# Moving half of the gate projection to the end of the in-projection, with the first attention pairs between its tiles

## The chip, the cores and the metric

The kernel runs on one core of one Trainium2 chip. The metric is the device time of one execution in microseconds. Three runs of the kernel before gave 1553.62, 1555.27 and 1555.58 us, so its median is 1555.27 us.

## The reference, cut to what matters

One layer of a diffusion backbone over 1024 latent and 256 context tokens (1280 in all), model width 1024. After adaLN modulation and RMSNorm, ONE input projection feeds two groups:

```python
p   = h @ w_in                                   # columns: q k v (3*512) | z (512) | a,b (16) | nq nk nv (3*512)
# group A, 4 heads of 128: gated DeltaNet, forward and backward scans summed
q, k, v = split(silu(conv5(p[q k v])))           # depthwise convolution over the tokens, 5 taps
q = l2norm(q) / sqrt(128);  k = l2norm(k)
v_new = u - w @ S;  o = (q*exp(g)) @ S + qk @ v_new;  S = S*exp(g_last) + k_dec.T @ v_new   # per chunk
oA = rmsnorm(o_f + o_b) * silu(z)                # z: the output gates
# group B, 8 heads of 64: neighbourhood attention, 8x16 window plus all context keys, one softmax
oB = softmax(rms(nq) @ rms(nk).T + bias) @ nv
x = x + gate * (concat(oA, oB) @ w_out);  then RMSNorm, SwiGLU, gated residual
```

The group A scans need q, k, v and, per chunk, an inverted triangular matrix; the gates z are wanted only when a chunk's two scans are both done.

## The kernel before, in words

All fp32 products are made of three fp32r products of split operands (`hi` and `lo` parts), so each logical product is three matmuls. `hh` and `hl` are the two parts of the normalised input, eight tiles of 128 x 1280 each, held in SBUF for the whole in-projection.

**The job list.** The in-projection is a list of jobs, run in order by the loop at line 1032. A `Block` (line 405) makes 128 output columns over all tokens, channel-major: 8 k-steps of 9 matmuls (6 where only latent tokens are wanted: `q` and `nq`). Its matmuls are recorded at line 402. Kinds `q`, `k`, `v` then go through `evac` (ScalarE copies to `cr` at line 450, five VectorE operations at lines 454 and 458 for the convolution), `silu` (line 465) and, one job later, `finish` (PE transposes at line 524, VectorE scaling into `vt` at line 528, a store to DRAM). Kinds `nq`, `nk` go through a norm (line 489 on). A `Wide` (line 561) makes 256 columns token-major, one tile of 128 tokens at a time, 24 matmuls a tile (line 585): `z` for the gates (8 latent tiles), `nv` for the attention's values (10 tiles). Its weights are fetched in two halves through one buffer `wraw`: a DMA (line 576), a ScalarE cast to `hi` (line 577), a GpSimd subtraction to `lo` (line 578).

The order before is `k0 k1 k2 k3 z1 | nk0 nk1 nk2 z0 nk3 | nq0 nq1 nq2 q0 q1 q2 q3 | nv0 v0 nv1 v1 v2 v3 nq3`.

**What runs beside the jobs.** `bg` steps two background pieces between k-steps and tiles: the block inverses (from the sixth job on), then `preps` (line 905), which prepares ten chunks for each scan direction. A prep loads `kk`, `xc`, `at` from DRAM, and is a chain over POOL `rg` (938), PE `pr` (948, 949), ACT `e` (952), DVE `kk` and `at` (955, 960), PE (967), ACT, then three rounds of PE (978), DVE and ACT copies into `y` (980, 981), and stores `y_d` and `at_d` (990). Only the first two chunks are prepared before all four `q` blocks are done (line 993 on). `bg2` steps the second modulation (64 loads `wad`, VectorE sums at line 234). After `nv1` the SyncE queue copies the values into the attention's layout, 64 DMAs `vw_d<-nv_d` (line 1082).

**The end of the list.** Before the last job (`nq3`) the remaining preps are drained into the program, the pools of the attention are opened, and the generator `attention` (line 253) is stepped once, which issues the loads of the first heads (lines 259 to 262), of the biases `bt` (271) and of the values. Its 32 pairs (line 284) each make scores on PE (302), max and exponentials (DVE 304, ACT 306, DVE 307 and 308), PE transposes (313) copied by ACT to `pt` (316), PE products with the values (323) and an ACT copy to `no` (325).

**The scans** (line 1163) run after the list: ten chunks in each direction, loads at line 1139, PE at 1170, 1180, 1189, 1201 and 1206, DVE and ACT between. After each step of a scan `beside(PACE)` steps the attention by 0.72 on average, so that its 32 pairs are spread over the scans. After the scans the output projection uses `w_out`, whose first two blocks are loaded and cast by `weights` (lines 195, 199, 200).

Each engine executes its instructions in the order of the program; that order is set at build time by a scheduler, not by the source's order alone. The gates' and values' ScalarE-issued stores use ScalarE's DMA queue; all other DMAs named here go through SyncE's (SP).

## Time and profile before

| | |
|---|---|
| median of three runs | 1555.27 us |
| the profiled execution | 1559.04 us |
| its span, first to last instruction | 1556.6 us |
| mean granted TensorE clock | 0.983 |
| TensorE busy | 1480.3 us, 95% |
| VectorE, ScalarE, GpSimd busy | 987.5, 723.6, 238.2 us |
| in-projection's last matmul / first scan matmul / last attention product | 574.3 / 597.2 / 822.8 us from the start |

The profiled execution took 2.4 us more than its span, and 3.8 us more than the median. Times in the text below are microseconds from the start of the span. Busy time counts each matmul from issue to its modelled end, and neighbours overlap; where the PE's idle time is named, no matmul was under way.

### The profile page before, as it was taken

To read this page: it belongs to the slowest core of one execution; us is meant where nothing else is said; L and a number is where in the kernel's file an instruction comes from. 1 tells how busy PE (TensorE), PEld (TensorE's weight loads), DVE (VectorE), ACT (ScalarE), POOL (GpSimd) and SP (SyncE) were. 2 spreads that over 40 slices of the span, in tenths; PEclk is the share of its full clock that TensorE was granted. 3 is DMA by queue.
4 is the path that set the end of the run, shared out by engine and by line. 5 is a ranking of instruction groups with operands and counts; after the bars stand their busy time and mean duration, and the time that the engine had idled before them with its cause. 6 is when DMAs were issued, how large, how long until landed. Compare 5 with 4: busy or idle time off the path is not lost. (4 is left out here: it accounts for less than half of the span.)

```text
span 1556.6 us, 23940 instructions
## 1 busy us (share of the span) xinstructions
PE 1480.3 (95%) x8702; PEld 1237.2 (79%) x8702; DVE 987.5 (63%) x1712; ACT 723.6 (46%) x1400; POOL 238.2 (15%) x286
## 2 busy tenths in 40 slices
PE   6999899999989987999899999999999999999998
PEld 3788787679888766887787878888888888888887
DVE  5774496674254755667786559856565656689652
ACT  5442553664343455665774256333333333454440
POOL 1154501633353320111210000000000000000000
PEclk9999999999999999999999999999999999999999
DMA  9274221677355568898737601633322224698742
GB/s 389 61 220 126 72 76 61 185 227 220 122 173 158 167 190 251 280 279 254 224 109 234 236 34 50 230 107 105 106 102 102 102 101 156 227 380 285 239 147 81
DMA packets 202423, 267.35 MB, mean 172 GB/s; under 512 B 16833, under 2 KB 112577, under 8 KB 201281
## 3 DMA queue, kind: packets, MB, share of 16 engines
q1 hardware_dynamic: 196688, 261.07, 51.5%
q10 hardware_dynamic: 5616, 4.76, 0.9%
q8 instruction: 68, 1.11, 0.3%
q14 instruction: 51, 0.41, 0.1%
HBM read 201.02 MB, written 68.94 MB: 173 GB/s over the span
## 5 line engine op out<-in xcount | busy, mean ns | idle before, releaser
L402 PE MATMUL blk<-hh,whi 128*128 128x512 f32 (+1 forms) x410 | 121.3, 390 | 1.4 <-ACT kk L547 1.4
L1387 ACT CAST uhi<-wq 128x512 fp32r<-128x512 f32 x101 | 61.0, 622 | 132.0 <-issue 84.6
L1387 ACT CAST uhi<-ws 128x512 fp32r<-128x512 f32 x91 | 53.9, 621 | 146.5 <-PE ps L1326 92.6
L402 PE MATMUL blk<-hh,wlo 128*128 128x512 f32 (+1 forms) x410 | 116.7, 378 | 0.6 <-POOL wlo L200 0.6
L402 PE MATMUL blk<-hl,whi 128*128 128x512 f32 (+1 forms) x410 | 115.6, 377 | 0.3 <-DVE hl L688 0.3
L1388 DVE TENSOR_TENSOR ulo<-wq,uhi 128x512 fp32r<-128x512 f32 x101 | 67.6, 688 | 58.8 <-ACT uhi L1387 32.5
L1326 PE MATMUL ps<-hT,uhi 128*128 128x512 f32 x336 | 103.6, 390 | 0.0
L1326 PE MATMUL ps<-lT,uhi 128*128 128x512 f32 x336 | 103.5, 389 | 0.0
L1326 PE MATMUL ps<-hT,ulo 128*128 128x512 f32 x336 | 103.5, 389 | 0.0
L1326 PE MATMUL ps<-hB,uhi 128*128 128x512 f32 x288 | 89.2, 391 | 0.6 <-ACT hB L1501 0.6
L1326 PE MATMUL ps<-lB,uhi 128*128 128x512 f32 x288 | 88.8, 389 | 0.4 <-DVE lB L1502 0.4
L1326 PE MATMUL ps<-hB,ulo 128*128 128x512 f32 x288 | 88.7, 389 | 0.0
L585 PE MATMUL blk<-zhi,hh 128*128 128x256 f32 (+1 forms) x288 | 84.5, 294 | 1.1 <-ACT kk L547 1.1
L402 PEld LDWEIGHTS blk<-hh,wlo 128*128 128x128 f32 x410 | 72.2, 191 | 15.4 <-POOL wlo L200 0.9
L402 PEld LDWEIGHTS blk<-hl,whi 128*128 128x128 f32 x410 | 72.4, 192 | 14.7 <-DVE hl L688 0.8
L585 PE MATMUL blk<-zhi,hl 128*128 128x256 f32 (+1 forms) x288 | 83.1, 288 | 0.0
L402 PEld LDWEIGHTS blk<-hh,whi 128*128 128x128 f32 x410 | 69.1, 191 | 16.4 <-issue 4.0
L585 PE MATMUL blk<-zlo,hh 128*128 128x256 f32 (+1 forms) x288 | 81.6, 283 | 0.0
L304 DVE CUSTOM_DVE_ANT_0 bt<-sc,bt 128x640 f32<-128x640 f32 x64 | 52.6, 822 | 34.6 <-PE sc L302 12.9
L1326 PEld LDWEIGHTS ps<-hT,ulo 128*128 128x128 f32 x336 | 63.1, 188 | 13.2
L1326 PEld LDWEIGHTS ps<-lT,uhi 128*128 128x128 f32 x336 | 63.1, 188 | 13.1
L1326 PEld LDWEIGHTS ps<-hT,uhi 128*128 128x128 f32 x336 | 62.9, 188 | 12.9
(360 smaller groups left out, 3645.9 us busy)
## 6 DMA issues: line engine op xcount, KB each, us to landing
wq<-w_fo SPq DMA_DIRECT2D x99, 256.0 KB, 4.3
wq<-w_gu SPq DMA_DIRECT2D x88, 256.0 KB, 2.8
wad<-wa SPq DMA_DIRECT2D x64, 256.0 KB, 3.9
bt<-rpb SPq DMA_DIRECT2D x64, 192.0 KB, 3.8
t_d<-g SPq DMA_DIRECT2D x22, 512.0 KB, 3.5
fr<-t_d SPq DMA_DIRECT2D x44, 256.0 KB, 5.1
f_d<-g SPq DMA_DIRECT2D x33, 256.0 KB, 2.1
fr<-f_d SPq DMA_DIRECT2D x33, 256.0 KB, 4.3
```

The costliest lines, as they stand in the source:

```text
L304: dve.tensor_tensor_reduce(bt, sc[:, u * 640:u * 640 + 640], bt, -1.0, 3.0e38, OP.add, OP.min, m[:, 0:1])
L402: pe.matmul(o, ww[:, k], xx[k][:, s], start=k == 0 and j == 0, stop=k == KT - 1 and j == 2)
L585: pe.matmul(p[:, :c1 - c0], x[k][:, s], ww[:, k, c0:c1], start=k == 0 and j == 0, stop=k == KT - 1 and j == 2)
L1326: pe.matmul(o, w[wi][:, k], x[xi][:, k], start=first and k == 0 and j == 0, stop=k == n - 1 and j == 2, skip_group_check=True)
L1387: act.copy(hi, self.raw[key])
L1388: dve.tensor_tensor(lo, self.raw[key], hi.bitcast(F32), OP.subtract)
```

## The change

The order becomes `k0 k1 k2 k3 z1 | nk0 nk1 nk2 nv0 nk3 | q0 q1 q2 q3 | nq0 nq1 nq2 nq3 v0 nv1 v1 v2 v3 z0`:

- `z0`, the first half of the gates, goes from the ninth place to the very end; `nv0` takes the ninth place.
- the four `q` blocks come straight after `nk3`, the four `nq` blocks behind them.
- the preps are drained, and the attention's pools opened and its first loads issued, before `v3` (now the last job but one).
- during `z0` the attention is stepped once after each of the 8 tiles, which is four of its 32 pairs; its PSUM pool is opened before `z0`, and `z0`'s tiles and the last transposes share that pool's two small banks. `PACE` goes from 0.72 to 0.63.
- `z0`'s weights live in a tile `zw` of the scans' pool, the place that `oacc` takes later. Its results go to `zg`, four tiles together, with one SiLU and one store for four.
- the columns are split 256 and 272 (256 gates and the 16 decay columns) where they were 264 and 264.

```diff
-PACE = 0.72
+PACE = 0.63
...
+            if len(psum) == 2:
+                return psum[1].tile([128, 512], F32, name=name, tag=name, bufs=4 if name == "blk" else 2)
+            return psum[2].tile([128, 512], F32, name=name, tag="ps", bufs=2)
...
-                self.n = 264 if kind == "z" else 256
+                self.n = 272 if kind == "z" and half else 256
+                self.lasting = kind == "z" and not half
+
+            def room(self):
+                w = self.zp().tile([128, 2, KT, 256 if self.lasting else 272], F32R, name="zw", tag="zw")
+                self.hi, self.lo = w[:, 0], w[:, 1]
...
+                    if half == 0:
+                        if t % 4 == 2:
+                            zg = cp.tile([128, NCH, 128], F32, name="zg", tag="kx", bufs=3)
+                            zg = zg.rearrange("p a b -> p (a b)")[:, :1024]
+                        act.copy(zg[:, (t - 2) % 4 * 256:(t - 2) % 4 * 256 + 256], p[:, :256])
+                        if t % 4 == 1:
+                            act.activation(zg, zg, AF.Silu)
+                            act.dma_start(z_d[(t - 5) * 128:(t - 1) * 128, 0:256].rearrange("(c p) d -> p c d", p=128),
+                                          zg.rearrange("p (c d) -> p c d", d=256))
+                        yield
+                        continue
...
-        jobs += [Block("nk", i) for i in range(3)] + [Wide("z", 0, zp), Block("nk", 3)]
-        jobs += [Block("nq", i) for i in range(3)] + [Block("q", 0)]
+        jobs += [Block("nk", i) for i in range(3)] + [Wide("nv", 0, zp), Block("nk", 3)]
         turn = len(jobs)
-        jobs += [Block("q", i) for i in (1, 2, 3)]
+        jobs += [Block("q", i) for i in range(4)]
         later = len(jobs)
-        values = later + 2
-        queries = range(turn - 1, later)
-        jobs += [Wide("nv", 0, zp), Block("v", 0), Wide("nv", 1, zp), Block("v", 1), Block("v", 2), Block("v", 3), Block("nq", 3)]
+        queries = range(turn, later)
+        jobs += [Block("nq", i) for i in range(4)] + [Block("v", 0), Wide("nv", 1, zp)]
+        values = len(jobs) - 1
+        jobs += [Block("v", i) for i in (1, 2, 3)] + [Wide("z", 0, zp)]
...
-            if n == len(jobs) - 1:
+            final = n == len(jobs) - 1
+            if n == len(jobs) - 2:
                 bg.drain()
                 bg2.drain()
                 late.close()
                 sp1 = pools(middle, "sp1", "left")
+                zpool[0] = sp1
+                jobs[n + 1].room()
                 fill = attention(pools(attn, "nw", "left", 2))
                 next(fill)
+            if final:
+                psa.close()
+                psum.append(scan_psum.enter_context(tc.tile_pool(name="psg", bufs=1, space=PSUM)))
...
                 for t, _ in enumerate(j.tiles()):
-                    next(fin, 0)
+                    if t > 1 or not final:
+                        next(fin, 0)
+                    if final:
+                        next(fill)
...
-    oacc = sp1.tile([128, 8, 4, 128], F32, name="oacc", tag="oacc")
+    oacc = sp1.tile([128, 8, 4, 128], F32, name="oacc", tag="zw")
```

How the instructions move, at three places. First, TensorE at the end of the in-projection. Before, the last block `nq3` ends (`blk`), ten transposes of `v3` (`m<-cst,cacc`) and the norm of `nq3` follow, and then the attention's first scores (`sc<-kh,qs`):

```order
L402 MATMUL blk<-hh_458,wlo 128x512 x2
L524 MATMUL m<-cst,cacc 128x128 x10
L489 MATMUL m<-cr,cst 128x512 x2
L302 LDWEIGHTS qs
L302 MATMUL sc<-kh,qs 128x256
```

Of the change, the same engine some thirty rows later: `v3` has ended, 16 score matmuls have gone (the last two are shown), then come two transposes of the first pair's probabilities (`sc<-cst,bt`), and only behind these the first gate matmuls (`blk<-zw`; `hh` with the `hi` half, `hl` with `hi`, `hh` with `lo`):

```order
L303 MATMUL sc<-kh,qs 128x384
L303 LDWEIGHTS qs
L303 MATMUL sc<-kl,qs 128x384
L314 MATMUL sc<-cst,bt 128x128 x2
L595 MATMUL blk<-zw,hh_129 128x256
L595 MATMUL blk<-zw,hl_130 128x256
L595 MATMUL blk<-zw,hh_129 128x256
L595 MATMUL blk<-zw,hl_130 128x256
L314 MATMUL sc<-cst,bt 128x128 x3
```

So the gates' tiles stand behind the first pair's softmax. Second, ScalarE at the same place of the change: the cast of the gate weights' first half, the copies of `v3` out of PSUM (`cr<-blk`), `v3`'s SiLU (which reads the finished convolution), a table load, the first exponential of the attention, and then the cast of the weights' second half:

```order
L587 CAST zw<-wraw 128x8x128
L453 COPY cr<-blk 128x256
L453 COPY cr<-blk 128x512 x2
L468 ACTIVATE cacc<-cacc 128x1280
L307 ACT_TABLE_LOAD
L307 ACTIVATE bt,mx<-bt,mx 128x640
L587 CAST zw<-wraw 128x8x128
```

Before, these gate casts stood some 150 rows earlier, and behind `v3`'s SiLU came the evacuation and norm of `nq3`. Third, ScalarE and the casts of the first two `w_out` blocks (`whi<-wraw`). Before, each stands alone among the scans, here the second of them, ahead of the scans' `vk` and of the finished chunks' scaling:

```order
L316 COPY pt<-sc 128x640
L199 CAST whi<-wraw 128x1024
L1193 ACTIVATE vk<-ps,KN 128x128 x4
L1247 ACTIVATE oacc<-z,orr 128x128 x4
L316 COPY pt<-sc 128x640
```

Of the change both stand at the head of the scans, ahead of the very first `vk`:

```order
L199 CAST whi<-wraw 128x1024
L326 COPY no<-sc 128x8x16
L199 CAST whi<-wraw 128x1024
L371 CAST na_5470<-no 128x512
L317 COPY pt<-sc 128x640
L307 ACTIVATE bt,mx<-bt,mx 128x640
L1218 ACTIVATE vk<-ps,KB 128x128 x4
```

Nothing of them is left in the middle of the scans; SyncE issues their two loads during the last tiles of `z0`, behind the fifth pair's biases.

More of the change, by code (lines that the diff above doesn't have):

```diff
@@ L184, in rsqrt, with weights @@
             dve.scalar_tensor_tensor(r, y, 1.5, r, op0=OP.add, op1=OP.mult)
-    def weights(wp, raws=2):
+    def weights(wp, raws=2, wide=132):
         def load(src, kt=KT, n=128, lo_engine=pool, raw=None, hi_engine=None):
@@ L189, in load @@
             if not given:
-                raw = wp.tile([128, KT, 132], F32, name="wraw", tag="wraw", bufs=raws)
+                raw = wp.tile([128, KT, wide], F32, name="wraw", tag="wraw", bufs=raws)
             hi = wp.tile([128, KT, 128], F32R, name="whi", tag="whi")
@@ L250, in hybrid @@
     attn = ctx.enter_context(ExitStack())
+    scan_psum = ExitStack()
     psum = []
@@ L377, in hybrid @@
         hp = pools(bs, "hp", "right")
-        load_w = weights(wp, 1)
-        early = ExitStack()
+        load_w = weights(wp, 1, 136)
+        early, psa = ExitStack(), ExitStack()
         psum.append(early.enter_context(tc.tile_pool(name="psb", bufs=8, space=PSUM)))
@@ L565, in __init__ @@
                 self.kind, self.half, self.zp = kind, half, zp
-                self.n = 264 if kind == "z" else 256
+                self.n = 272 if kind == "z" and half else 256
[3 more added lines that the diff above has]
+                self.hi, self.lo = w[:, 0], w[:, 1]
             def prefetch(self):
                 h2, n = 2 * self.half, self.n // 2
-                src = a["w_z" if self.kind == "z" else "w_nv"]
-                self.hi = self.zp().tile([128, KT, 264], F32R, name="zhi", tag="zhi")
-                self.lo = self.zp().tile([128, KT, 264], F32R, name="zlo", tag="zlo")
+                src = a["w_nv"] if self.kind == "nv" else a["w_z%d" % self.half]
+                if self.kind == "z":
+                    h2 = 0
+                if not self.lasting:
+                    self.room()
                 for i in range(2):
-                    raw = wp.tile([128, KT, 132], F32, name="wraw", tag="wraw", bufs=1)
+                    raw = wp.tile([128, KT, 136], F32, name="wraw", tag="wraw", bufs=1)
                     r, s = raw[:, :, :n], slice(i * n, i * n + n)
@@ L602, in tiles @@
                         for j, (ww, x) in enumerate(((self.hi, hh), (self.hi, hl), (self.lo, hh))):
-                            pe.matmul(p[:16, :CT], ww[:, k, 248:264], x[k][:, :CT], start=k == 0 and j == 0,
+                            pe.matmul(p[:16, :CT], ww[:, k, 256:272], x[k][:, :CT], start=k == 0 and j == 0,
                                       stop=k == KT - 1 and j == 2)
-                    abT = cp.tile([16, CT], F32, name="abT", tag="abT")
-                    act.copy(abT, p[:16, :CT])
+                    abT = cp.tile([16, 272], F32, name="abT", tag="zt", bufs=2)
+                    act.copy(abT[:, :CT], p[:16, :CT])
                     yield
-                nz = 264 if half == 0 else 248
                 for t in range(2, NCH):
-                    p = self.wide(t, 0, 264)
-                    if half == 1 and t == 3:
+                    p = self.wide(t, 0, self.n)
+                    if half == 0:
[9 more added lines that the diff above has]
+                        continue
+                    if t == 3:
                         q = bank()
```

26 lines of the change are left out of this document (11 added, 15 removed).

## The prediction

> **What bounds the kernel now.** I read the page's busy times first, then the engines' busy times in the stretches around the change, then TensorE's own timeline and its waits there.
>
> ```profile
> PE 1480.3 (95%) x8702; PEld 1237.2 (79%) x8702; DVE 987.5 (63%) x1712; ACT 723.6 (46%) x1400; POOL 238.2 (15%) x286
> ```
>
> TensorE is busy 95% of the span and every other engine at most 63%. The change takes no matmul away and adds none: 192 gate, 240 value matmuls and the 32 pairs only change places. So the time can change only by TensorE's idle time and by the stretches in which its clock is halved. The stretches (length, then busy time of PE, PEld, DVE, ACT, POOL, granted clock, DMA share, GB/s):
>
> ```profile
> 486.40:574.30 87.90, 82.23 (x566) 66.24 (x565) 52.99 (x65) 35.05 (x71) 30.56 (x42) 1.00 0.50 155
> 574.30:585.60 11.30, 5.45 (x31) 3.10 (x30) 6.32 (x14) 10.00 (x14) 0.00 (x0) 1.00 0.71 205
> 585.60:597.20 11.60, 9.11 (x60) 6.55 (x60) 5.01 (x13) 5.49 (x11) 1.54 (x4) 0.71 0.90 282
> 597.20:822.80 225.60, 208.15 (x1934) 182.90 (x1933) 161.04 (x486) 151.24 (x417) 34.56 (x69) 0.97 0.74 228
> ```
>
> The in-projection's second half is 82.2 of 87.9 busy, the scans 208.2 of 225.6; the worst places are the 11.3 us behind the last block (5.45 busy, so 5.85 idle) and the 11.6 before the first scan matmul (2.5 idle, clock 0.71). TensorE's rows show why:
>
> ```profile
> 574.33 1.04 PE L524 MATMUL m<-cst,cacc 128*128 128x128 f32 x8
> 576.52 1.98 PE L489 MATMUL m<-cr,cst 128*128 128x512 f32 x4 [0.36 <-ACT cr L468]
> 579.28 0.27 PE L302 MATMUL sc<-kh,qs 128*128 128x256 f16 x1 [0.78 <-ACT cr L490]
> 585.63 0.78 PE L313 MATMUL sc<-cst,bt 128*128 128x128 f32 x5 [3.81 <-DVE mx L307]
> ```
>
> After v3's transposes and nq3's norm it has the first scores only, and then waits 3.81 us for the first pair's softmax on VectorE. Half the clock follows each of the three longest waits of this part. The clock's column in short windows shows it, with the two waits inside the scans beside it:
>
> ```profile
> 586.20:593.00 6.80, 5.65 (x35) 4.13 (x34) 2.23 (x6) 3.24 (x7) 0.67 (x2) 0.50 0.84 248
> 709.00:716.00 7.00, 6.16 (x38) 4.87 (x36) 4.75 (x16) 3.90 (x8) 1.00 (x3) 0.51 0.53 155
> 750.00:757.00 7.00, 6.17 (x34) 5.59 (x36) 5.36 (x16) 4.60 (x13) 0.00 (x0) 0.51 0.44 139
> 704.66 1.05 ACT L199 CAST whi<-wraw 128x1024 fp32r<-128x1024 f32 x1 [1.74 <-DMA wraw<-w_out]
> 708.38 0.74 PE L313 MATMUL sc<-cst,bt 128*128 128x128 f32 x5 [2.67 <-DVE bt L308]
> 747.87 1.04 ACT L199 CAST whi<-wraw 128x1024 fp32r<-128x1024 f32 x1 [3.33 <-DMA wraw<-w_out]
> 750.83 2.07 PE L1206 MATMUL ps<-vk,kt 128*128 128x128 f32 x8 [4.08 <-DVE vn L1195]
> ```
>
> Each stretch is about 6.8 us at 0.50 or 0.51. The two inside the scans have one cause: ScalarE stands before a cast of `w_out` whose DMA has not come (1.74 and 3.33 us), everything behind that cast on ScalarE is late, and TensorE goes idle 2.67 and 4.08 us. Last, the waits of TensorE for the block inverses' and the preps' chains from 406 to 574:
>
> ```profile
> PE pr L967 <- DVE y L980: 5.6, 3, 2.6
> PE pr L967 <- DVE kk L955: 4.8, 4, 3.8
> PE pr L978 <- DVE y L980: 2.4, 1, 2.4
> PE pr L978 <- POOL y L958: 0.7, 1, 0.7
> PE pr L978 <- ACT e L952: 0.3, 1, 0.3
> ```
>
> Together 5.6 + 4.8 + 2.4 + 0.7 + 0.3 = 13.8 us.
>
> **The change part by part.** All sums are against the profiled execution's 1559.04 us.
>
> (a) **From v3's last matmul to dense gate matmuls.** v3 is now followed by its own convolution with nothing in front of it. Its operations, by the same tile's rows for nq3 and v3 (min/median/max in ns, the shapes behind):
>
> ```profile
> L458 DVE SCALAR_TENSOR_TENSOR cacc<-cr,cw,cacc x8: 483/874/1284, 557.6 to 567.1; 128x254 f32<-128x254 f32 x2, 128x255 f32<-128x255 f32 x2, 128x1022 f32<-128x1022 f32 x2, 128x1023 f32<-128x1023 f32 x2
> L454 DVE TENSOR_SCALAR cacc<-cr,cw x2: 332/562/791, 557.2 to 559.8; 128x256 f32<-128x256 f32 x1, 128x1024 f32<-128x1024 f32 x1
> L450 ACT COPY cr<-blk x3: 373/592/592, 554.9 to 559.0; 128x512 f32<-128x512 f32 x2, 128x256 f32<-128x256 f32 x1
> ```
>
> On VectorE that is 0.33 + 0.79 for L454, 4 x 0.48 for the narrow and 4 x 1.28 for the wide L458, 8.2 us; the program keeps the first pair's max behind it. I take 7.6, since part runs while the last copies come, and 0.4 for the first copy. Before, nq3's matmuls (573 us and earlier) covered this convolution whole. Then on ScalarE, by these groups:
>
> ```profile
> L465 ACT ACTIVATE cacc<-cacc 128x1280 f32<-128x1280 f32 x1 | 1.3, 1275 | 2.6 <-DVE cacc L458 2.6
> L306 ACT ACTIVATE bt<-bt,mx 128x640 f32<-128x640 f32 x5 | 4.1, 827 | 0.0
> L199 ACT CAST whi<-wraw 128x1024 fp32r<-128x1024 f32 x1 | 1.0, 1047 | 0.0
> L490 ACT ACT_TABLE_LOAD x1 | 1.3, 1283 | 0.0
> L578 POOL TENSOR_TENSOR zlo<-wraw,zhi 128x1024 fp32r<-128x1024 f32 x4 | 10.2, 2562 | 51.6 <-ACT zhi L577 51.6
> ```
>
> v3's SiLU 1.3, a table load 1.3, the first exponential 0.8 and its sum 0.1, then the cast of the gate weights' second half 1.05, and on GpSimd its `lo` part 2.56. The order leaves this chain serial: 0.4 + 7.6 + 1.3 + 1.3 + 0.9 + 1.05 + 2.56 = 15.1 us, beside which TensorE has some 1.9 us of scores: 13 idle, where there were 5.85. **+7.2**. Bounds: 0, where the scheduler's first gate tile needs less of this than I read (the first k-steps need only the weights' first half, cast earlier), to +9, where nothing at all stands beside the 15.1 (less 5.85). The half clock after it was there before: no difference.
>
> (b) **The gate tiles.** Eight tiles share two PSUM banks with v2's and v3's transposes, and ScalarE copies each out and makes two SiLUs, each with a table load there and one back, 4 x 1.28 = 5.1 us between exponentials on which pairs wait. The nearest measured wait of pairs for exponentials is small (0.78 us at 579.28), and a tile is 24 matmuls to hide under. **+2**; bounds 0 (all hidden) to +5 (all four loads exposed).
>
> (c) **From the last gate tile to the first scan matmul.** v3's last transposes are issued among the gate tiles, so the store `v_d` and the load `v` come late:
>
> ```profile
> v_d<-vt SPq DMA_DIRECT2D x4, 640.0 KB, 5.2
> v<-v_d SPq DMA_DIRECT2D x16, 256.0 KB, 4.7
> ```
>
> What a pair holds in TensorE's work, by the attention's scores, transposes and products alone from 597 to 823:
>
> ```profile
> 597.00:823.00 226.00, 43.21 (x290) 28.36 (x290) 0.97 0.74 228
> 597.00:823.00 226.00, 45.67 (x300) 33.48 (x300) 0.97 0.74 228
> 597.00:823.00 226.00, 46.26 (x618) 36.21 (x615) 0.97 0.74 228
> ```
>
> At ten transposes a pair the 300 of the second row are 30 pairs: 135.1 / 30 = 4.5 us each. The store and the load are 5.2 + 4.7 us, with some 2 us of scaling before them 12; beside them stand about one and a half pairs, 6.8 us. So 5.2 idle where there were 2.5: **+3**, rounded up for the products that wait themselves; bounds 0 and +7, which is the store and the load wholly bare (9.9 less 2.5).
>
> (d) **`w_out` out of the middle of the scans.** Both casts move ahead of the first scan step, and their loads are issued during the gates. The idles go, 2.67 + 4.08 = 6.75, and with them two half-clock stretches, 2 x 3.4: **-13.5**. What is late next there is the attention's own softmax, whose waits are inside the other 10.7 us idle of the scans and stay. Bounds -13.5 to 0 (a DMA that is late at the new place blocks ScalarE at the scans' start instead).
>
> (e) **The preps.** From the third chunk on they ran beside nv0, v0, nv1, v1, v2, v3 and the drain before nq3; now they run beside nq2, nq3, v0, nv1, v1, v2, with one more block ahead of them. The `nq` and `nk` blocks give VectorE no convolution, and the waits above were for DVE in all but 1.0 us. I halve them: **-7**; bounds -13.8 and +4. The other end counts that the four `q` blocks' convolutions now all lie together with preps 0 and 1 and the modulation's sums, worth one wait of the longest kind (3.8 us).
>
> (f) **SyncE's queue.** Behind nv1 come the 50 copies of the values, and the preps' stores behind those:
>
> ```profile
> 482.08 34.60 SPq L1082 DMA_DIRECT2D vw_d<-nv_d  x50
> 565.45 0.44 SPq L259 DMA_DIRECT2D qs<-nq_d  x1
> 572.10 0.94 SPq L271 DMA_DIRECT2D bt<-rpb  x2
> bt<-rpb SPq DMA_DIRECT2D x64, 192.0 KB, 3.8
> ```
>
> 34.6 us before, 0.69 each. Before, nv1 was followed by v1, v2, v3 and nq3; now only by v1, v2 and v3 before the heads are wanted. From the last prep's stores to the heads' loads (ten loads from 565.45 to 571.5, 6 us) and the first bias (+3.8) is about 10 us. In the order of the change the last prep's matmuls stand 33 matmuls before v3's end (its last three k-steps and six transposes); at the stretch's mean, 82.23 / 566 = 0.145, that is 4.8 us, and two thirds of them are of the longest kind, so I take 6. Hence the biases arrive 4 to 9 us behind v3's end, together with the convolution of (a): **0**; bounds 0 to +8.
>
> The sum: 7.2 + 2 + 3 - 13.5 - 7 + 0 = **-8.3**: 1550.7, and the median stood 3.8 below the profiled execution, so **1547 us**.
>
> [...] The table load first:
>
> ```profile
> 576.49 1.28 ACT L490 ACT_TABLE_LOAD   x1
> 577.78 1.45 ACT L490 ACTIVATE cr<-m,bias 128x512 f32<-128x512 f32 x2
> ```
>
> The activation behind the load starts 0.01 us after the load's end. [...] The half clock next: the three stretches above last about 6.8 us, and one follows an idle of 2.67 us. [...]
>
> **The rivals.**
>
> A, **SyncE's queue becomes the bound: slower.** If the last prep ends with v3's matmuls and not 6 us before, then stores, heads and biases come 8 us after the convolution of (a), TensorE stands idle that long, and the preps, which then end in a drain without cover, save nothing. Price: +8 and (e) at 0, so -8.3 + 7 + 8 = +6.7: **1562**. It decides from about 8 us of lateness on. For it: three blocks in place of four behind nv1, and 50 copies of 0.69 us that are as many as before. Against it: before, the copies ended at 516.7, and the first head's load was issued at 565.45 without hurry; the 49 us between them is more than nq3's share, some 11 us, which is what the new order takes away.
>
> B, **the gates start at once: more gain.** If the first gate tile is not held by the weights' second half, and the convolution hides beside gate matmuls, (a) and (b) vanish: -17.5: **1538**. For it: the first half of the weights is cast early, and 192 matmuls wait there. Against it: the first gate matmuls stand behind the first transposes of pair 1.
>
> C, **the change does not do what it says.** The preps' waits come back in full beside other blocks, since their chain is bound to its own DVE and PE steps and not to what lies beside it: -8.3 + 7 = -1.3: **1554**.
>
> **How the numbers follow.** My forecast has 0.40, with a range of its own from 1542 to 1552; A has 0.29, B 0.17, C 0.14. A median that differs by 0.2%, 3.1 us, is about what a measurement of this kernel can tell from no change, so C counts as "same", A as slower, and the forecast and B as faster, 0.57. The range has to take in most of A and B as well, so it reaches some 4 us past the centre of each, 1534 to 1567: 4 us are what (c) can be worse than I took it (+7 for +3), and about half of what (e) can be better. What lies beyond, (a), (c) and (f) all at their bad ends, or B with all of the preps' waits gone, I hold for less than 0.2.
>
> **What would show it.** (a): from v3's last `blk` matmul to the first run of 24 gate matmuls, 15 us with some 13 idle, TensorE released by POOL's `lo` part or by the softmax; if it is released by a DMA (`bt`, `kh`, `qs`), it is A. (b): gate tiles that wait for ACT copies or exponentials, 2 us in all. (c): a wait of 5 us for the DMA `v` before the first L1170-like scan matmul. (d): no cast of `w_out` with a wait behind 620 us, and no clock of 0.5 in the scans. (e): the waits of the preps' `pr` at 7 us, where 13.8 again means C. My forecast is wrong if the window between v3's end and the first scan matmul, less the gates' own work, is over 20 us, or if the scans still hold a stretch at half clock.

## The result: no gain

The change took 1557.17 us (median of 12 runs), the kernel before 1555.28 (12 runs beside them): ratio 1.0006, 95% interval 0.9987 to 1.0025. A second set of twelve runs gave 1559.24 against 1556.81, 1.0015 (1.0004 to 1.0027). So the change is not faster in either set, and in the second it is slower by 0.15%. The forecast was 1547.

The profiled execution took 1556.61 us with a span of 1554.8. Its page:

```profile
PE 1486.3 (96%) x8702; PEld 1239.4 (80%) x8702; DVE 993.5 (64%) x1712; ACT 727.8 (47%) x1404; POOL 234.1 (15%) x286
```

6.0 us more busy time than before, with the same 8702 matmuls, and a span 1.8 us shorter: so 7.8 us less idle time, and matmuls that took longer in sum. The stretches of the change (columns as before: length, busy time of PE, PEld, DVE, ACT, POOL, granted clock, DMA share, GB/s), from nk3's end on, and then two stretches in which the clock was halved:

```profile
249.40:394.40 145.00, 133.43 (x749) 106.68 (x750) 88.51 (x106) 70.95 (x121) 60.04 (x64) 0.93 0.61 188
394.40:556.30 161.90, 151.95 (x1102) 125.83 (x1096) 79.05 (x96) 81.11 (x157) 62.30 (x80) 0.97 0.51 159
556.30:573.10 16.80, 6.09 (x27) 3.80 (x26) 12.44 (x20) 7.30 (x13) 3.07 (x4) 0.56 0.96 263
573.10:608.90 35.80, 35.78 (x316) 34.01 (x316) 12.21 (x29) 16.17 (x30) 1.77 (x6) 0.97 0.46 133
608.90:620.70 11.80, 7.87 (x53) 6.10 (x51) 5.50 (x12) 9.50 (x16) 2.20 (x4) 0.71 1.03 338
620.70:820.20 199.50, 194.89 (x1827) 170.92 (x1827) 153.69 (x463) 138.41 (x394) 30.50 (x62) 1.00 0.73 235
257.90:268.10 10.20, 10.20 (x45) 8.68 (x44) 3.00 (x2) 3.40 (x8) 0.00 (x0) 0.50 0.17 66
558.30:575.40 17.10, 8.35 (x36) 6.08 (x37) 11.75 (x19) 6.74 (x10) 2.62 (x2) 0.50 0.91 247
```

The gates themselves (573.1 to 608.9, with the pairs between their tiles) leave no idle time, 35.78 of 35.80. The scans are 4.6 us idle in 199.5, where they were 17.4 in 225.6, and in this execution never at half clock. But v3's end is followed by 16.8 us with 6.09 busy, and by 17.1 us at half clock (558.3 to 575.4), where before there had been 6.8 behind the list's end. TensorE's rows there, and at the first scan matmul:

```profile
561.22 0.58 PE L303 MATMUL sc<-kh,qs 128*128 128x256 f16 x2 [4.90 <-DMA kh<-nk_d]
567.45 0.37 PE L303 MATMUL sc<-kh,qs 128*128 128x256 f16 x1 [3.60 <-DVE mx L305]
570.61 0.66 PE L314 MATMUL sc<-cst,bt 128*128 128x128 f32 x2 [1.93 <-DVE bt L309]
573.12 0.80 PE L595 MATMUL blk<-zw,hh 128*128 128x256 f32 x2
...
620.73 1.13 PE L1214 MATMUL ps<-v,y 128*128 128x128 f32 x8 [1.33 <-DMA y<-y_d]
```

It waits 4.90 us for the keys of the first heads, 3.60 for a maximum, 1.93 for the scaled exponentials. SyncE's queue and ScalarE at that time:

```profile
550.82 0.80 SPq L1009 DMA_DIRECT2D y_d<-y  x2
553.76 0.62 SPq L260 DMA_DIRECT2D qs<-nq_d  x1
561.43 0.94 SPq L272 DMA_DIRECT2D bt<-rpb  x2
563.61 0.60 SPq L586 DMA_DIRECT2D wraw<-w_z  x1
```

```profile
564.33 1.27 ACT L468 ACTIVATE cacc<-cacc 128x1280 f32<-128x1280 f32 x1 [7.02 <-DVE cacc L461]
567.47 1.28 ACT L307 ACT_TABLE_LOAD   x1 [1.87 <-DVE mx L305]
569.59 1.03 ACT L587 CAST zw<-wraw 128x1024 fp32r<-128x1024 f32 x1
```

The last prep's store goes at 550.8, the heads from 553.8 to 561, the biases at 561.4; the second half of the gates' weights (`wraw<-w_z`) only at 563.6, and its cast stands behind the first exponential, as the order said. VectorE's first maximum starts at 566.57, 2.34 us after v3's convolution, and was released by the bias `bt`.

**By stage.** Below, idle is a stretch's length less PE's busy time. Lost is an estimate of what the half clock cost: half of PE's busy time inside the stretches at half clock (the change's gate matmuls of 256 columns start 0.21 us apart at half clock, 573.71 to 573.92, and 0.12 us apart from 575.64 on, at full clock). (The scans' stretch ends 0.6 us sooner here than in the rows above, hence 16.9 for 17.4.) Two profiled executions of each kernel (the second ones are the runs e1 and e5):

| us, idle + lost | before | before, again | change | change, again |
|---|---|---|---|---|
| up to nk3's end | 23.0 + 3.4 | 20.7 + 1.7 | 21.6 + 4.9 | 22.6 + 3.4 |
| seven blocks q0 to q3, nq0 to nq2 | 8.4 + 7.6 | 10.7 + 3.4 | 11.6 + 10.1 | 12.1 + 8.3 |
| to the end of the last block | 13.8 + 3.3 | 13.8 + 5.0 | 10.0 + 4.9 | 9.4 + 3.3 |
| to the first scan matmul | 8.3 + 2.8 | 8.3 + 2.8 | 14.7 + 7.0 | 17.8 + 5.1 |
| to the attention's end | 16.9 + 6.0 | 15.5 + 4.7 | 4.5 + 0 | 3.4 + 3.8 |
| the rest | 5.9 + 0 | 5.9 + 0 | 6.1 + 0 | 7.6 + 0.8 |
| sum (rounded apart) | 76.3 + 23.2 | 74.9 + 17.7 | 68.5 + 26.9 | 72.9 + 24.7 |

On the mean the change has 4.9 us less idle time and loses 5.3 more to the half clock, so the two cancel. The mean spans differ by 2.5 us (1554.1 and 1556.6); the other 2 us are busy time that neither column holds (PE's busy time less lost: 1457.1 and 1459.0 before, 1459.4 and 1460.8 of the change). Two executions of one kernel differ by up to 4.0 us in a row of this table (26.4 and 22.4 in the first), so a difference of 2 us in one row is no more than a hint.

**The clock over the runs.** Every run lists its mean granted clock. Over 94 runs of the kernel before, in four sets, the median was 0.985 each time; over the change's 24 runs it was 0.9795 and 0.980. In the change's first twelve runs the time follows the clock (correlation -0.96, 1.1 us for each 0.001):

| clock | 0.978 | 0.978 | 0.979 | 0.981 | 0.982 | 0.986 | 0.990 |
|---|---|---|---|---|---|---|---|
| us | 1561.38 | 1560.21 | 1556.61 | 1555.59 | 1553.84 | 1548.97 | 1547.44 |

At before's 0.985 the fitted line gives 1551.7 for these twelve runs, but the change rarely has that clock. In its other twelve runs (e5) the tie is looser: correlation -0.75, 0.9 us for each 0.001, and 1555.2 at 0.985.

### The profile page after: what moved, and what is told of

Read it like the earlier page. It is cut to its first block, busy times and chain, and to the rows that moved or that the text cites. A ratio compares the mean times of both kernels' runs of the same rounds, so it can differ in the third digit from the quotient of the medians.

```text
span 1554.8 us, 23965 instructions
## 1 busy us (share of the span) xinstructions
PE 1486.3 (96%) x8702; PEld 1239.4 (80%) x8702; DVE 993.5 (64%) x1712; ACT 727.8 (47%) x1404; POOL 234.1 (15%) x286
## 5 line engine op out<-in xcount | busy, mean ns | idle before, releaser
L595 PE MATMUL blk<-zw,hh 128*128 128x256 f32 (+1 forms) x576 | 115.2, 294 | 0.9 <-ACT kk L550 0.8
L595 PEld LDWEIGHTS blk<-zw,hh 128*128 128x128 f32 x576 | 93.0, 193 | 4.7 <-issue 2.0
L405 PEld LDWEIGHTS blk<-hh,wlo 128*128 128x128 f32 x410 | 72.7, 193 | 15.4 <-POOL wlo L200 0.9
L405 PEld LDWEIGHTS blk<-hl,whi 128*128 128x128 f32 x410 | 72.9, 193 | 14.5 <-DVE hl L707 0.8
L595 PE MATMUL blk<-zw,hl 128*128 128x256 f32 (+1 forms) x288 | 83.5, 290 | 0.0
L200 POOL TENSOR_TENSOR wlo<-wraw,whi 128x1024 fp32r<-128x1024 f32 x18 | 45.3, 2517 | 180.6 <-ACT whi L199 173.2
```

Source lines behind the costliest of these rows:

```text
L200: lo_engine.tensor_tensor(o, r, h.bitcast(F32), OP.subtract)
L405: pe.matmul(o, ww[:, k], xx[k][:, s], start=k == 0 and j == 0, stop=k == KT - 1 and j == 2)
L595: pe.matmul(p[:, :c1 - c0], x[k][:, s], ww[:, k, c0:c1], start=k == 0 and j == 0, stop=k == KT - 1 and j == 2)
```

## The experiments

All ratios are to runs of the kernel before on the same chip, with 95% intervals. e1 to e4 ran together, e5 to e8, e9 to e11, and e12 to e14; each of these four sets had a chip of its own. Ratios inside a set compare directly. Across sets they are less sure than their intervals: e10 and e14 are one kernel, and came out 0.6% apart.

**e1, the kernel before again.** No edit.

> The kernel before, unchanged. Theory H (half clock decided by a grid): the time is TensorE's work, its idle time and what the half clock adds, and the half clock falls in steps of 3.41 us on a grid that is not tied to the program, so it differs from execution to execution. Expected: idle near 76 us as in the first profile, some of the half-clock stretches at other places or of other length than before, the two behind the late output weights at 709 and 750 still there, and a time that follows the mean clock over the runs. Rival P (the program alone decides): the same nine stretches within 1 us of their places, and a time that does not follow the clock.

1555.14 us, 0.9992 (0.9976 to 1.0009). Idle 74.9 against 76.3. Three of its half-clock stretches:

```profile
583.80:590.60 6.80, 5.66 (x35) 4.19 (x35) 2.15 (x6) 3.29 (x7) 0.67 (x2) 0.50 0.90 245
706.60:713.40 6.80, 5.96 (x36) 4.70 (x35) 4.74 (x16) 3.91 (x8) 0.81 (x3) 0.50 0.58 169
747.60:751.00 3.40, 3.40 (x17) 3.04 (x16) 2.28 (x9) 2.63 (x8) 0.00 (x0) 0.50 0.69 238
```

They stand behind the same waits as before (the program is shifted by 2 to 3 us here), but the last is 3.4 us long where it was 6.8, and over the execution 17.7 us were lost and not 23.2. So the waits belong to the program, and what the half clock adds to them to the execution.

**e2, the output weights early, alone.** In the kernel before:

```diff
+        ws = [weights(wp)(a["w_out"][b], lo_engine=dve) for b in range(2)]
         for d in range(2):
             load(d, ORDER[d][0], (ORDER[1 - d][1],))
...
-    ws = [load_w(a["w_out"][b], lo_engine=dve) for b in range(2)]
```

> Before, with the loads and casts of the first two output weights written ahead of the first scan step, nothing else. Theory H: the two waits of TensorE inside the scans (2.67 + 4.08 us) go with their two half-clock stretches (3.0 each by the records): 12.7 us less, 0.992. Rival (the gain is given back later: the pairs reach another wait, or the early load collides with the heads' and biases' loads at the attention's start): 0.997 or more.

1548.41 us, 0.9954 (0.9933 to 0.9974): -7.3 where 12.7 were expected. The two stretches, and the scans' first wait:

```profile
576.40:597.70 21.30, 11.49 (x71) 7.54 (x69) 10.77 (x20) 14.15 (x21) 0.62 (x2) 0.84 0.88 264
597.70:815.50 217.80, 207.08 (x1952) 182.03 (x1952) 161.55 (x492) 151.58 (x419) 34.57 (x70) 0.98 0.78 236
598.30:605.10 6.80, 5.52 (x27) 5.26 (x26) 1.26 (x3) 3.15 (x13) 0.00 (x0) 0.50 0.78 243
```

```profile
PE ps L1189 <- DMA y<-y_d: 3.3, 2, 2.0
```

The scans' idle time falls from 16.9 to 10.7, and no stretch at half clock is left at 700 or 750. But the scans' first steps now wait 3.3 us for `y`, 1.5 us more idle time stands before the scans, and a new half-clock stretch of 6.8 us follows. Nearly half of the expected gain is missing, and a loss stands at the scans' start. That the two early weights in the queue cause that loss is argued, not shown: the first `y` load is issued 15.0 us behind the list's end, before it was 16.3.

**e3, the q blocks first, alone.** In the kernel before:

```diff
-        jobs += [Block("nq", i) for i in range(3)] + [Block("q", 0)]
-        jobs += [Block("q", i) for i in (1, 2, 3)]
+        jobs += [Block("q", i) for i in range(4)]
+        jobs += [Block("nq", i) for i in range(3)]
```

> Before, with the four q blocks moved ahead of nq0 to nq2, nothing else, so that the preps start three blocks sooner. Theory H, from the profile of the change: the preps' waits of 13.8 us fall by 5 to 7, the q blocks cost 3 us more idle, and the clock of that stretch is a lottery of +-3: 0.998, within 0.996 to 1.001. The prediction's term (e) alone would give -7 us: 0.9955.

1551.43 us, 0.9975 (0.9956 to 0.9993): the size that was expected, for another reason:

```profile
240.70:382.20 141.50, 129.57 (x738) 104.83 (x736) 94.95 (x111) 74.43 (x124) 63.73 (x66) 0.95 0.64 196
382.20:575.50 193.30, 179.36 (x1358) 156.42 (x1357) 86.66 (x107) 78.79 (x159) 64.78 (x80) 0.97 0.52 161
599.60:816.40 216.80, 206.14 (x1915) 178.26 (x1913) 160.02 (x484) 149.09 (x412) 34.99 (x69) 0.99 0.72 225
```

The preps' stretch still has 193.3 - 179.4 = 13.9 us idle (13.8 before), and since the preps start sooner, some of their waits now lie ahead of that stretch: in all, TensorE waits 17.1 us for them (the `pr` rows from 330 us on), where before it waited 13.8. Starting them three blocks sooner saved nothing. The gain is in the scans (10.7 idle, not 16.9): with the other order the scheduler had put the first cast of the output weights at 597.6, ahead of the scans, and the second waited 1.54 us. So e2 and e3 have part of one gain in common.

**e4, the change with the gates' weights ahead of the heads.**

```diff
                 jobs[n + 1].room()
+                jobs[n + 1].prefetch()
                 fill = attention(pools(attn, "nw", "left", 2))
...
-            if n + 1 < len(jobs):
+            if n + 1 < len(jobs) and n != len(jobs) - 2:
                 jobs[n + 1].prefetch()
```

> The change, with both loads of z0's weights issued ahead of the heads' loads, so that the gates' matmuls stand right behind v3 and the first pair's softmax behind them. Theory H: of the 10.4 us idle between v3 and the dense gates and the 4.2 us of half clock there some 10 go: 0.9935 against the change, 1547 us. Rival A (SyncE's queue): the heads come later by the two loads and the idle moves behind the gates' first tiles or to the first scan step: 0.998 or more against the change.

1553.02 us, 0.9978 (0.9960 to 0.9997): 4 to 6 us below the change's two ratios, half of what was expected. The gates now go first, but still wait for the weights:

```profile
559.51 0.58 PE L595 MATMUL blk<-zw,hh 128*128 128x256 f32 x1 [4.64 <-ACT zw L587]
562.47 0.80 PE L595 MATMUL blk<-zw,hh 128*128 128x256 f32 x2 [1.73 <-POOL zw L588]
```

4.64 + 1.73 us for the cast and its `lo` part, where the change waits 10.4 for heads and softmax; then the tiles run, and the softmax lies beside them. Neither theory held in full.

**e5, the change again.** No edit.

> The change, unchanged. Theory H: its idle time again near 68.5 us, 6 to 8 below before; its median clock below before's 0.985, near 0.980, and the time over its runs follows the clock by some 1.1 us for each 0.001; the 17 us stretch at half clock behind v3 there again, shorter or longer by one or two steps of 3.41 us. Rival N (the clock is noise of one chip or one profile, and the change saves no idle time): clock as before's, idle within 2 us of before's.

Time and clock are given above and are as theory H has them. The idle time is not: 72.9, only 2.0 to 3.4 below before's two profiles, of which 4.5 are one wait at the first scan step:

```profile
619.32 2.05 PE L1214 MATMUL ps<-v,y 128*128 128x128 f32 x8 [4.51 <-DMA y<-y_d]
```

The half clock behind v3 lasts 17.1 us again, and 3.8 us are lost inside the scans, where the first profile of the change had none.

**e6, e2 and e3 together.**

> Before with the two parts together that were measured alone (-7.3 and -4.3 us on the same chip): output weights early and the q blocks first; z0 stays the ninth job and nq3 the last. Theory S (the parts add, and the loss of the change lies in z0 at the end): 0.993, 1545 us. Rival (the preps' saving and the early output weights use the same slack, or the clock takes it back): 0.996 or more.

1546.47 us, 0.9935 (0.9918 to 0.9952): by the ratios the two nearly add (-0.46% and -0.25%, in another set).

```profile
380.10:571.50 191.40, 177.81 (x1358) 154.86 (x1357) 86.35 (x107) 78.87 (x159) 64.88 (x80) 0.98 0.53 162
594.10:808.40 214.30, 204.32 (x1928) 179.74 (x1928) 159.47 (x486) 149.24 (x415) 33.86 (x68) 0.99 0.74 228
```

Preps 13.6 idle, scans 10.0. By idle time they do not add: the scans have 10.7, 10.7 and 10.0 in e2, e3 and e6, and what e6 has beyond them is half clock (14.6 us lost in its profile, 18.7 and 20.6 in theirs). Two parts of the change, without the gates at the end, gain 10 us; the whole change (e5, in the same set) gains none.

**e7, the change kept warm with narrow matmuls.** Ahead of the first pair's scores:

```diff
+                if not warmed:
+                    warmed.append(u)
+                    for _ in range(40):
+                        pe.matmul(sc[:, 1408:1536], hh[0][:, :128], hh[0][:, :128], start=True, stop=True)
```

> The change with 40 matmuls of 128 x 128 added that nothing uses (into 128 columns of the first pair's PSUM tile that hold nothing), ahead of the first scores, where TensorE waits 4.9 us for the heads. Idle time alone as the cause: the scores come no earlier and the time stays or grows by up to 0.5 us. Theory H: the window behind v3 is then over half busy, the 17 us stretch at half clock starts later or not at all, and the 4.2 us that it costs fall to 2 or less: 0.9985 against the change, 2 us.

1558.73 us, 1.0011 (0.9998 to 1.0023): nothing gained. TensorE had the added matmuls under way and the clock was halved all the same:

```profile
554.14 6.46 PE L296 MATMUL sc<-hh 128*128 128x128 f32 x40 [1.03 <-ACT cr L458]
```

```profile
553.30:556.70 3.40, 2.56 (x23) 2.56 (x23) 3.33 (x6) 0.79 (x2) 0.27 (x2) 1.00 0.95 274
556.70:573.80 17.10, 12.56 (x59) 10.63 (x58) 10.35 (x17) 6.74 (x10) 2.62 (x2) 0.50 0.87 233
```

2.56 of the 3.40 us ahead of the half clock were busy. So busy time by the records did not hold the clock here. Ahead of the half clock 23 of these matmuls took 2.56 us, 0.11 us each for 128 columns (all 40 took 6.46, 0.16 on the mean); e9's, below, took 5.73 / 24 = 0.24 us each for 512.

**e8, no pairs between the gates' tiles.**

```diff
-PACE = 0.63
+PACE = 0.72
...
-                    if final:
-                        next(fill)
```

> The change with the attention not stepped between z0's tiles and the pace back at 0.72 (the first pair's scores stay where they are, the scheduler may still fill with what is ready). If the pairs between the tiles are what makes the gates' stretch dense: the four pairs cost 18 us of TensorE's work in the scans instead, where 4.7 us are idle, so the time is 0 to +4 us against the change. If they cost the start of the attention its wait (the gates stand behind the softmax because of them): -5 us or more.

1562.56 us, 1.0034 (1.0020 to 1.0047), 3.3 us above the change beside it. The wait behind v3 is as it was (5.01 us for the heads, then 3.75 and 1.94): the pairs did not cause it. Between the tiles they seem to be worth those 3 us, though the two intervals overlap.

**e9, kept warm with wide matmuls.** As e7, with 24 matmuls of 512 columns:

```diff
+                    for _ in range(24):
+                        pe.matmul(sc[:, 1024:1536], hh[0][:, :128], hh[0][:, :512], start=True, stop=True)
```

> As the run with 40 idle matmuls of 128 columns, but with 24 of 512 columns (into 512 columns of the first pair's PSUM tile that the second head's scores overwrite later). Theory H2 (the clock is held by the columns that stream through the array, not by matmuls being under way: the 128-column ones took 0.167 us each, of which 128 columns at 0.45 ns are a third): the stretch at half clock behind v3 begins two steps later or not at all, 2 to 4 us less than the change, ratio to before 0.999 to 1.000. Rival (the clock is halved by something else, so nothing run there holds it): the 17 us stretch stays, and the time is that of the change, 1.001 or more.

1555.15 us, 0.9980 (0.9965 to 0.9994): faster than before, and 0.3% below the change's two ratios (other sets; its interval meets that of 1.0006 and lies clear of that of 1.0015), with 24 matmuls more that nothing uses. Its median clock is 0.986 where the change had 0.980.

```profile
553.58 5.73 PE L296 MATMUL sc<-hh 128*128 128x512 f32 x24 [1.03 <-ACT cr L458]
```

```profile
557.90:561.30 3.40, 2.53 (x19) 1.94 (x18) 2.63 (x3) 0.60 (x1) 0.00 (x0) 1.00 1.10 221
564.70:571.50 6.80, 4.54 (x20) 4.09 (x21) 4.86 (x10) 4.44 (x9) 2.62 (x2) 0.50 0.67 215
```

The half clock behind v3 falls from 17.1 to 6.8 us, starts behind the next wait, and costs 2.3 us where it cost 4.2 and 5.1. The stretch from 557.9 is 2.53 us busy, no more than the 2.56 ahead of e7's half clock, and the clock stays full. The scores came no sooner, so in this profile part of the price of that wait was the clock and not the wait.

**e10, e6 with nv0 and z0 exchanged** (nv0 ninth as in the change, z0 ahead of v0).

> Before with the output weights early, the q blocks first, and nv0 and z0 exchanged (nv0 the ninth job, z0 ahead of v0): of the three moves of the gates this one alone. Theory H (the rest of the change's loss is half clock in the stretch of the inverses, since in all five profiles with nv0 in the ninth place the wait for the inverses leaves 10.2 us at half clock and 15 us of lost work up to the last nq, where the others have 7): 1551 to 1553, 0.996. Rival (that stretch is as before, and the loss lies at the end): 1546.5, 0.9935.

1540.90 us, 0.9891 (0.9870 to 0.9912). Theory H expected a loss here, and has fallen on this point; the time lies below the rival's too. The stretch up to nq2 loses 4.9 us to the half clock, and the preps' stretch is better than in the runs so far:

```profile
391.00:566.00 175.00, 168.34 (x1276) 146.75 (x1275) 80.64 (x102) 82.90 (x159) 58.83 (x78) 0.98 0.57 171
```

175.0 - 168.3 = 6.7 idle. That looks like the prediction's halving, but 3.3 us of the preps' waits lie ahead of this stretch: in all (the `pr` rows from 330 us on) TensorE waits 9.7 us for them, where e6 waits 15.4. The two kernels differ by the exchange of nv0 and z0, so it is the exchange that gives it, not the earlier start.

**e11, e6 with nq3 behind nq2,** so that v3 is the last block.

> Before with the output weights early, the q blocks first, and nq3 right behind nq2, so that v3 is the last job, with nothing behind it that hides its convolution; z0 stays ninth. The prediction's term (a) by itself: v3's convolution and SiLU, 9 us, stand bare before the scans and beside the first pair's softmax: 5 to 8 us more than the same kernel with nq3 last (1546.5), 0.997 to 0.999. Rival (the first pair's softmax does not wait for the convolution on VectorE, and the heads come sooner): within 2 us of 1546.5, 0.9935 to 0.9945.

1552.61 us, 0.9965 (0.9950 to 0.9980), 0.3% above e6's ratio, which is of another set and whose interval just meets this one. The convolution with nothing to hide it, in one row:

```profile
585.46 1.97 PE L524 MATMUL m<-cst,cacc 128*128 128x128 f32 x8 [8.47 <-ACT cacc L465]
```

v3's transposes wait 8.47 us for its SiLU, behind five VectorE operations.

**e12, the change with nq3 between v3 and z0.**

```diff
-        jobs += [Block("nq", i) for i in range(4)] + [Block("v", 0), Wide("nv", 1, zp)]
+        jobs += [Block("nq", i) for i in range(3)] + [Block("v", 0), Wide("nv", 1, zp)]
-        jobs += [Block("v", i) for i in (1, 2, 3)] + [Wide("z", 0, zp)]
+        jobs += [Block("v", i) for i in (1, 2, 3)] + [Block("nq", 3), Wide("z", 0, zp)]
```

> The change with one block moved: nq3 goes back behind v3, so that the list ends v3, nq3, z0, and v3's convolution lies beside nq3's matmuls. Theory H3 (what the change loses against the run with z0 ahead of v0 is what stands bare behind v3, with the half clock that follows it): some 6 us less than the change, as the same move cost without the gates, 1551 to 1552, 0.997. Rival (the first gate tile waits for the second half of its weights and for the pair's softmax whatever the last block is): the gap moves behind nq3 and the time is that of the change, 1.000 to 1.0015.

1548.38 us, 0.9954 (0.9937 to 0.9972): 0.5 to 0.6% below the change's two ratios (8 to 9 us where 6 were expected), with one block moved, though in another set. TensorE behind the last block:

```profile
556.00 0.27 PE L303 MATMUL sc<-kh,qs 128*128 128x256 f16 x1 [1.01 <-ACT cacc L438]
560.38 0.37 PE L303 MATMUL sc<-kh,qs 128*128 128x256 f16 x1 [3.12 <-DVE mx L305]
563.38 0.66 PE L314 MATMUL sc<-cst,bt 128*128 128x128 f32 x2 [1.78 <-DVE bt L309]
```

1.01 + 3.12 + 1.78 us where the change had 4.90 + 3.60 + 1.93. The heads are there when the last block ends. (The profile is of the slowest of its six runs, 1553.75 us at a clock of 0.980.)

**e13, e12 with e4's edit.**

> Both repairs at the end of the list: nq3 between v3 and z0, and z0's weights issued ahead of the heads. Theory H3: the two costs add (6 and 4 us), 1546 to 1548, 0.9935, level with the run of the two parts without any gates at the end. Rival (they are one cost, hidden by either): no better than the weights alone, 0.9975.

1548.20 us, 0.9949 (0.9936 to 0.9963), level with e12: the two repairs do not add, nor is it the rival's 0.9975. The gates wait again, for the buffers that nq3's copies hold (the last of these copies stands behind a cast that waits 1.94 us for the second half of the weights):

```profile
549.98 0.39 PE L595 MATMUL blk<-zw,hh 128*128 128x256 f32 x1 [4.01 <-ACT cacc L438]
```

**e14, e10 again.** No edit.

> The kernel that was fastest so far (output weights early, q blocks first, nv0 ninth, z0 ahead of v0), unchanged. Expected 1541 to 1545 us, 0.989 to 0.992, a clock of 0.987 to 0.991. The theory that the order nv0, nk3, q0 brings a long stretch at half clock behind the inverses expects 10 us of it near 254; if it has 3.4 to 6.8 us again, that theory has fallen.

1547.20 us, 0.9950 (0.9934 to 0.9967), not 0.9891, and outside what was expected: the two intervals do not meet, though it is the same kernel, with a median clock of 0.9865 in place of 0.989. Its stretches:

```profile
249.60:392.00 142.40, 128.93 (x700) 104.07 (x700) 87.52 (x102) 70.01 (x117) 58.48 (x62) 0.92 0.63 191
392.00:576.00 184.00, 177.47 (x1340) 153.56 (x1340) 86.57 (x108) 88.69 (x167) 65.99 (x83) 0.98 0.56 170
258.20:265.00 6.80, 6.80 (x34) 6.01 (x34) 1.30 (x1) 3.22 (x8) 0.00 (x0) 0.50 0.09 34
```

The preps' stretch is good again (184.0 - 177.5 = 6.5 idle, and again 9.7 us of waits for the preps in all), but up to nq2 the half clock costs 11.9 us where e10 had 4.9. The stretch behind the inverses is 6.8 us, between the change's 10.2 and e10's 3.4. So its length is not the order's alone. The two sets differ by chip as well, and nothing here tells chip from chance. The best that can be said of e10, e14, e6, e12 and e13 is that all lie 0.5 to 1.1% below before; which is best is open.

## Why the prediction was wrong

Its sum was -8.3. By its steps, against the means of the two profiles of each kernel (idle and lost together):

- **(a), (b), (c), the start of the attention**: +12.2 forecast, +11.2 measured (22.3 against 11.1). The order was read rightly: v3's convolution with nothing to hide it, the softmax and the second half of the weights behind it. That the sum came so near is partly luck: the forecast was idle time alone, the measured part is 8.0 idle and 3.3 half clock. (b) was nothing, not +2. The table load cost what was taken for it: it starts at 567.47, lasts 1.28, and the exponential starts at 568.76. "The half clock after it was there before: no difference" does not hold: 17.1 us in place of 6.8, which e9 takes back. In (c) the scans waited for `y` (1.33 and 4.51 us), not for `v`. The test that the prediction set itself was missed: from v3's end to the first scan matmul there are 64.4 us, and 28.6 without the 35.8 in which the tiles run, not 20. What it costs to leave v3's convolution with nothing behind it is not shown by itself: e11 and e12 point the same way (0.3% and 0.5 to 0.6%), but both compare across sets. What e12 does show is that the three waits fall from 10.4 us to 5.9.
- **(d), the output weights**: -13.5 forecast, -15.7 measured in the scans, which also have some four pairs less to fit in. The two half-clock stretches had cost 6.0 by the records, not 6.8. In e2, where the casts alone moved, the same stretch gains 8.0, and the whole kernel 7.3.
- **(e), the preps**: this is the step that failed. "I halve them: -7" has its own sign in the prediction, the waits of the preps' `pr`: 7 us if it is right, 13.8 if rival C is. They are 10.5 and 10.2 in the two profiles of the change. The rows of the first:

```profile
PE pr L997 <- ACT kk L989: 3.5, 2, 2.9
PE pr L997 <- DVE y L999: 2.9, 2, 2.7
PE pr L986 <- DVE kk L974: 1.8, 3, 1.3
PE pr L986 <- DVE y L999: 1.7, 2, 1.5
PE pr L997 <- ACT y L1000: 0.6, 2, 0.3
```

So 3.4 us went, half of what was forecast, and other losses took them in the same part of the list: idle and half clock in the preps' stretch and the seven q and nq blocks ahead of it come to +1.9 together in place of -7 (-1.8 idle, +3.7 half clock, all of the latter in the q and nq blocks). That is a miss of 8.9 us, about the whole forecast gain. The q blocks stood in the sum with nothing but as a bound of +4. The reason for the halving was wrong too. With the q blocks first and z0 still ninth the waits are 17.1 (e3), 15.4 (e6) and 13.3 (e11). Over the sixteen profiles they go by which `Wide` stands ninth: 13.3 to 17.1 in the six with z0 there, 9.1 to 10.5 in the ten with nv0 there, whether z0 runs beside the preps (e10, e14) or behind them (the change). So what helped was that nv0 left the preps' side, which the prediction did not name; why nv0 hinders them, no run shows.

- **What no step held**: +1.9 ahead of nk3's end, nearly all half clock, where nothing changes but nv0 for z0 near the end of the stretch; +1.4 behind the attention; and the 2 us of busy time named above. All three are of the size by which two executions of one kernel differ.
- **(f) and rival A**: the biases came 10.3 us behind v3's end, where 4 to 9 were forecast, and so 2.3 us behind the convolution: a quarter of A's price. By the sign that the prediction gave A, a release by `kh` or `bt`, A did occur (4.90 us for `kh` on TensorE, 2.34 for `bt` on VectorE), but the first of these lies beside the convolution, which ended later. Rival B did not occur.

The time came out where rival C put it, within 0.2%, and that is not C's mechanism: C left the preps' waits whole, and a quarter of them went. The idle time did fall, by 4.9 us, and the clock took it. Taking "3.8 below" off as a constant was a mistake of the same kind: the profile of before was an execution that lost 23.2 us to the half clock, where the next lost 17.7.

Of the second test, a stretch at half clock in the scans, the first profile of the change shows none and the second 3.8 us lost.

The forecast took the 6.8 us of one profile as the length of a stretch at half clock. The traces show others: the nine whole stretches inside before's span are 3.41 or 6.83 us long, the nine inside the change's 3.41, 6.83, 10.24 or 17.07, and e11 has one of 13.7 (580.3 to 594.0): one to five times 3.41. In both traces their starts lie whole numbers of such steps apart as well: before's last three inside the span, at 586.18, 709.06 and 750.02, are 122.88 and 40.96 us apart, 36 and 12 steps. Where a stretch starts is not the program's alone: 2.0 us behind v3's end in the change, 3.6 us in e5, which are one kernel. A length of 6.8 in one profile is then a draw, not a price: the stretch near 750 lasted 6.8 us in the first profile of before and 3.4 in the second. Nor did waits of one length go ahead of them: before's stretch at 709 followed one of 2.67 us, the change's at 302.3 none at all (below).

What stays open: how much of the change's lower clock (0.980 against 0.985) is the order's, stage by stage. Behind v3 the profiles show it (17.1 us at half clock in the change, e5, e7 and e8, against 6.8 in e9 and 10.2 in e12, of each of which there is one). In the q and nq blocks 8.3 to 11.9 us were lost in the seven profiles of the change, e4, e5, e7, e8, e9 and e12, 6.8 in e13, and 4.9 and 11.9 in e10 and e14, which are one kernel; with z0 ninth (before, e1, e2, e3, e6, e11) it was 3.4 to 8.5. The means are 9.1 and 6.0, so the order with nv0 ninth leans to the lower clock, but no run separates order from chance.

## What to carry to other kernels

Before a block is moved to the end of a list, ask whose tail it was hiding: here nq3 hid v3's convolution. With nq3 put back behind v3 the kernel was 0.5% faster than before (e12, e13), where the change in its two sets was no faster. Write a forecast of a TensorE-bound kernel in two columns, idle time and time at half clock, and take the second from several executions: a median clock of 0.980 in place of 0.985 weighs about as much as 5 us of idle time here. Count a chain's waits by the rows of the chain, from its start, and not by the idle time of a stretch that the change itself shifts: e10's 6.7 us of idle time were 9.7 us of waits.

## What the runs showed of the hardware

Matmuls under way were not enough to hold the clock. In the change the 3.40 us ahead of 302.3 have no idle time at all, and the clock is halved behind them. Most of what ran there is narrow: of 33 matmuls, eight are products of 32 columns and sixteen of one column.

```profile
298.90:302.30 3.40, 3.40 (x33) 2.83 (x32) 0.46 (x2) 1.61 (x5) 2.87 (x11) 1.00 0.27 99
302.30:305.70 3.40, 3.40 (x27) 2.49 (x26) 0.42 (x1) 1.14 (x4) 0.02 (x1) 0.50 0.00 0
299.56 1.95 PE L486 MATMUL m<-ones,cr 128*128 128x1 f32 x16
```

At one place in the program, and with equal busy time, the clock was halved behind 128-column matmuls (e7, 2.56 of 3.40 us busy) and stayed full behind 512-column ones with the scores after them (e9, 2.53 of 3.40), in one profile each. So in these profiles PE's busy time alone did not tell where the clock would be halved.
